# Turn between two blocks: the last down projection in two column halves, row factors applied through a diagonal matrix

## The chip, the cores and the metric

One core of one Trainium2 chip. The metric is the device time of one execution in microseconds (us); lower is better. The kernel before took 1072.19 us, the median of 3 runs (1071.92 to 1072.72).

## What is computed

Two blocks over 256 tokens of 1024 channels, in fp32. The first ends in a mixture of experts (32 experts, two per token) that adds to the residual h, and in a final normalization; the second block begins with a normalization of its own and one wide projection:

```python
# end of the first block
    out = out + jnp.einsum('nef,efd->nd', h * combine[:, g, :, None], w_down[g])
    h = h + hierarchical_moe(hn, ...)
return rmsnorm(h, final_norm_g)
# start of the second block
    h = rms_norm(x, g_mix[l])
    z = jnp.einsum("bsd,de->bse", h, w_in[l]) + b_in[l]
    va, ga, xb, gb, sa, sb = jnp.split(z, cuts, axis=-1)
```

Both normalizations are taken of the same h: the first one's factor is needed for the residual, and the factor of both together for the projection's input.

## The kernel before

The tokens lie in two row blocks of 128 (index c), as h[128, 2, 1024]. The experts are worked off in 16 pairs; each pair takes 12 weight tiles of 1 MB (4 gate, 4 up, 4 down) from a ring of buffers in six pools (a to f), which SyncE (SP) fills in the order of use as soon as a slot is freed (`Ring`, L35 to L89). Of the last down tile, the two halves of columns are separate transfers (L128).

For a pair, TensorE computes gate and up (L830), VectorE and ScalarE form hs (L705), four transposes turn it (L713), and the down projection (L960 to L966) runs k = 0 to 3 outside, the two halves of 512 columns n = 0, 1 inside, into the banks dn0 and dn1. An fp32 matmul stands as two instructions in the trace, a transpose as one. `evac` (L720) writes the result of a half as a high part y[:, 0] (ScalarE) and a low part y[:, 1] (VectorE). `to_token` (L725) multiplies them by the one-hot matrix GT, two matmuls per row block and half, and VectorE adds the result to h. For the pairs before the last this is done inside the next pair.

After the last pair comes the turn. `scattered(c, n)` (L992) adds half n of the columns to row block c; `square` (L996, ScalarE) squares it with a sum per row in s1; `weighted` (L999, VectorE) multiplies the squares by g2, the broadcast of the first norm's squared gains (plus epsilon), with a sum per row in s2; `factor(c)` (L1002) adds the two sums on VectorE (sn) and takes the power -1/2 on GpSimd (r1). Then hn = h * r1 is written for both row blocks: for c = 0 by ScalarE (L1036) and VectorE (L1040), for c = 1 by VectorE in two halves (L1122). Sixteen transposes of hn (L1130) fill four PSUM banks, and `split_x` (L1078) makes from each the high part n_hi (ScalarE, L1082) and the low part n_lo (VectorE, L1085) of the projection's input X. r0 (L1123) is the first norm's own factor, with which h is scaled at L1136 by gfin, the broadcast of the gains (L1119).

The projection (`ws`, L1088) reads its weights in units, half a tile each: `Units.split` (L213) makes w_hi on ScalarE (L228) and, in the second block up to unit 75, w_lo on GpSimd (L229). Unit 0 is split in two pieces inside the turn (L1028, L1033, L1041), unit 1 at L1120, units 2 and 3 at L1137; later ones three units ahead of their use, in four buffers. A unit is 24 matmuls; the first two projections read units 0, 1 and 2, 3. PSUM has eight banks named acc here (L1048), given out in turn.

Order. From the end of the last pair's down projection (L969) to L1142 the instructions of TensorE, VectorE, ScalarE and GpSimd stand in the order of the code (`manual_schedule`). Before it, from the third pair on, this holds for TensorE alone (L929); after it a planner orders all engines by simulated times. SP's transfers follow the frees of the ring.

Of the kernel before, what the change touches and what calls it, by code (L numbers as in the profile page):

```python
# [8 lines left out]
F32 = mybir.dt.float32  # L9
# [3 lines left out]
AF = mybir.ActivationFunctionType  # L13
OP = mybir.AluOpType
# [78 lines left out]
def kernel(ctx: ExitStack, tc: tile.TileContext, a: dict, out):  # L93
    nc = tc.nc
    V, S, T, G = nc.vector, nc.scalar, nc.tensor, nc.gpsimd
# [3 lines left out]
    small = ctx.enter_context(tc.tile_pool(name="small", bufs=2))  # L99
    NA, NB, NC, ND, NE, NF = 5, 9, 2, 2, 1, 2  # L100
    R = ctx.enter_context(tc.tile_pool(name="R", bufs=1, side="right"))
    ring = Ring(nc)
# [14 lines left out]
    W_EXP = []  # L117
# [46 lines left out]
    h = keep.tile([128, 2, 1024], F32, name="h")  # L164
# [10 lines left out]
    ident = consts.tile([128, 128], F32, name="ident")  # L175
# [10 lines left out]
    def keep_warm(n, pool, name):  # L186

        p = pool.tile([128, 512], F32, name=name)
        for _ in range(n):
            T.matmul(p, ones_b, ones_b[:, 0:1].to_broadcast([128, 512]), start=True, stop=True)  # L190

    keep_warm(12, psA, "acc")
    mhalf = consts.tile([128, 4], F32, name="mhalf")
# [85 lines left out]
    r1 = small.tile([128, 2], F32, name="r1")  # L279
    diag = p1.tile([128, 2, 128], F32, name="diag", tag="x40")  # L280
# [16 lines left out]
    for kk in range(4):  # L297
        for kt in (2 * kk, 2 * kk + 1):
            S.activation(hnh[kt // 4][:, kt % 4], pts[kt // 2][:, kt % 2].rearrange("p c t -> p (c t)"), AF.Copy,
                         scale=gcol[:, kt:kt + 1])  # L300
        for kt in (2 * kk, 2 * kk + 1):
            V.scalar_tensor_tensor(hnl[kt // 4][:, kt % 4], pts[kt // 2][:, kt % 2].rearrange("p c t -> p (c t)"),
                                   gcol[:, kt:kt + 1], hnh[kt // 4][:, kt % 4].bitcast(F32), op0=OP.mult,
                                   op1=OP.subtract)
# [355 lines left out]
    def output(tag="r4"):  # L660
        return R.tile([128, 2, 512], F32R, name="y", tag=tag)
# [26 lines left out]
    def slots(i):  # L688
        g = GS[i].rearrange("t c j s -> t c (j s)")
        p = psM.tile([128, 2, 128], F32, name="ms")  # L690
        for c in range(2):
            T.transpose(p[:, c], g[:, c], ident)
        GT[i] = mw.tile([128, 2, 128], F32R, name="onehotT")
        S.activation(GT[i], p, AF.Copy)
        p = psM.tile([128, 3], F32, name="ms")
        for c in range(2):
            T.matmul(p, g[:, c], cwr[:, c, i], start=c == 0, stop=c == 1)
        CW[i] = mw.tile([128, 2], F32, name="cw")
        done = V.tensor_copy(CW[i][:, 0:1], p[:, 2:3])
        for j in range(2):  # L700
            s = slice(64 * j, 64 * j + 64)
            V.tensor_mul(CW[i][s, 1:2], p[s, j:j + 1], CW[i][s, 0:1])
        return done
# [9 lines left out]
    def transpose_h(hs, m, hT):  # L713
        p = psM.tile([128, 4, 128], F32, name="ms")
        for k in range(4):
            turned[0] = T.transpose(p[:, k, :m], hs[:m, k], ident[:m, :m])  # L716
        V.tensor_copy(hT[:, :, :m], p[:, :, :m])
        return hT

    def evac(dn, n, m, y):  # L720

        S.activation(y[:m, 0], dn[n][:m], AF.Copy)  # L722
        V.tensor_sub(y[:m, 1], dn[n][:m], y[:m, 0].bitcast(F32))  # L723

    def to_token(gt, c, m, y):  # L725

        p = psM.tile([128, 512], F32, name="ms")
        for k in range(2):
            T.matmul(p, gt[:m, c], y[:m, k], start=k == 0, stop=k == 1)  # L729
        return p  # L730
# [185 lines left out]
    def broadcast(p, rows, n):  # L916

        for k in range(4):
            T.matmul(p[:, k], ident[:, 4 * n + k:4 * n + k + 1].to_broadcast([128, 128]), rows, start=True, stop=True)
        return p.rearrange("p k c -> p (k c)")  # L920

    prev = None
    turn = ExitStack()
    steady = ExitStack()
    for i in range(16):
        if i == 2:


            steady.enter_context(tc.manual_schedule(engines={T.engine}))  # L929
        gate = psE.tile([128, 512], F32, name="gate")  # L930
        up = psE.tile([128, 512], F32, name="up")
        if i < 15:
            onehot(i + 1)
        products(i, "w_gate", gate, XG[i])
        if prev:
            scatter_late(*prev)
        if i == 0:
            with tc.issue_after(slots(0).ins):
                param_cols()
        with tc.issue_after(tile_done[0].ins) if i == 0 else ExitStack():  # L940
            products(i, "w_up", up, XG[i], (lambda: scatter(prev[0], prev[1], 1, 128)) if prev else None)
        if i == 0:
            nb = nc.values_load(nmore_i[0:1, 0:1], min_val=0, max_val=7)
        hs_hT = hidden()
        hs = act_mul(gate, up, CW[i], 128, hs_hT[:, 0])
        rows = gather(i + 1) if i < 15 else iter(())
        next(rows, None)
        if i < 2:
            next(rows, None)
            slots(i + 1)  # L950
        hT = transpose_h(hs, 128, hs_hT[:, 1])
        if 2 <= i < 15:
            next(rows, None)
            slots(i + 1)
        if i == 15:

            with tc.issue_after(turned[0].ins):
                g2 = [broadcast(psE.tile([128, 4, 128], F32, name=n), gfin_rows2, k) for k, n in enumerate(("gate", "up"))]
        dn = [psE.tile([128, 512], F32, name=f"dn{n}") for n in range(2)]
        for k, idx in enumerate(W_EXP[i]["w_down"]):  # L960
            t = ring.get(idx)
            for n in range(2):
                for j in range(2):
                    m = T.matmul(dn[n][64 * j:64 * j + 64], hT[:, k, 64 * j:64 * j + 64], t[:, j, 512 * n:512 * n + 512],  # L964
                             start=k == 0, stop=k == 3, skip_group_check=True)
            ring.free(idx)  # L966
        if i == 15:
            steady.close()
            turn.enter_context(tc.manual_schedule(engines={T.engine, V.engine, S.engine, G.engine}))  # L969
        y = output()  # L970
        evac(dn, 0, 128, y)
        prev = (GT[i], y, dn, 128)
        if i == 1:
            scatter_late(*prev)
            scatter(GT[i], y, 1, 128)
            prev = None
            overflow()
    y2 = output("r2")
    evac(dn, 1, 128, y2)

    s1 = small.tile([128, 2, 2], F32, name="s1")
    s2 = small.tile([128, 2, 2], F32, name="s2")
    floor = small.tile([128, 1], F32, name="floor")
    V.memset(floor, 1024 * EPS * EPS)
    sn = small.tile([128, 2], F32, name="sn")
    r0 = small.tile([128, 2], F32, name="r0")
    r1 = small.tile([128, 2], F32, name="r1")
    sqs = [R.tile([128, 2, 512], F32, name=f"sq2{c}", tag=("r3", "r1")[c]) for c in range(2)]  # L990

    def scattered(c, n):  # L992
        s = slice(512 * n, 512 * n + 512)
        V.tensor_add(h[:, c, s], h[:, c, s], to_token(prev[0], c, 128, (y, y2)[n]))

    def square(c, n):  # L996
        S.activation(sqs[c][:, n], h[:, c, 512 * n:512 * n + 512], AF.Square, accum_out=s1[:, c, n:n + 1])

    def weighted(c, n):  # L999
        V.scalar_tensor_tensor(sqs[c][:, n], sqs[c][:, n], 1.0, g2[n], op0=OP.mult, op1=OP.mult, accum_out=s2[:, c, n:n + 1])  # L1000

    def factor(c):  # L1002
        V.scalar_tensor_tensor(sn[:, c:c + 1], s2[:, c, 0:1], s2[:, c, 1:2], floor, op0=OP.add, op1=OP.add)
        G.tensor_tensor(r1[:, c:c + 1], sn[:, c:c + 1], mhalf[:, 0:1], op=OP.pow)

    ring.close("b")
    ring.close("c")
    ring.close("d")
# [10 lines left out]
                  + [(W_2[j], half) for j in (14, 15) for half in range(2)])  # L1019
    U = {unit: u for u, unit in enumerate(units2.seq)}  # L1020

    hn = q0.tile([128, 2, 1024], F32, name="hn", tag="t8")
    scattered(0, 0)
    square(0, 0)
    scattered(0, 1)
    square(0, 1)
    weighted(0, 0)
    low = units2.split(2)  # L1028
    scattered(1, 0)
    square(1, 0)  # L1030
    scattered(1, 1)
    square(1, 1)
    low.pop(0)()  # L1033
    weighted(0, 1)
    factor(0)
    S.activation(hn[:, 0, 512:1024], h[:, 0, 512:1024], AF.Copy, scale=r1[:, 0:1])  # L1036
    weighted(1, 0)
    weighted(1, 1)
    factor(1)
    V.tensor_scalar(hn[:, 0, 0:512], h[:, 0, 0:512], r1[:, 0:1], None, op0=OP.mult)  # L1040
    for step in low:  # L1041
        step()
    phase.close()


# [71 lines left out]
                nc.sync.dma_start(w[p0:p0 + hi - lo, :, c0:c0 + 96], src)  # L1117

    gfin = [broadcast(psP.tile([128, 4, 128], F32, name="acc"), gfin_rows, n) for n in range(2)]  # L1119
    units2.prep(1)  # L1120
    for n in range(2):
        V.tensor_scalar(hn[:, 1, 512 * n:512 * n + 512], h[:, 1, 512 * n:512 * n + 512], r1[:, 1:2], None, op0=OP.mult)  # L1122
    V.tensor_add(r0, s1[:, :, 0], s1[:, :, 1])  # L1123
    rms_scale(r0, r0, 1024)
    pt = [psP.tile([128, 2, 2, 128], F32, name="acc") for kk in range(4)]
    for c, kks in ((0, (2, 3, 0, 1)), (1, range(4))):
        for kk in kks:
            for k in range(2):
                kt = 2 * kk + k
                T.transpose(pt[kk][:, k, c], hn[:, c, 128 * kt:128 * kt + 128], ident)  # L1130
    for kk in range(4):
        split_x(X, pt[kk], PC["g_mix"], kk)
    for c in range(2):
# [384 lines left out]
```

## Time and profile before

| | us |
|---|---|
| median of 3 runs | 1072.19 |
| the profiled execution | 1072.1 |
| its span, first to last instruction | 1070.4 |
| TensorE busy in it | 1031.7 (96%) |
| VectorE busy | 544.5 (51%) |
| ScalarE busy | 369.3 (34%) |
| GpSimd busy | 221.4 (21%) |

TensorE's mean granted clock is 0.985 of full speed. The experts take the span from about 120 to 580 us, the turn lies at 570 to 596, the second block behind it. In the rows PE is a matmul on TensorE, PEld its weight load, DVE is VectorE, ACT ScalarE, POOL GpSimd, SPq the queue of SyncE. Times are us from the start of the span unless marked ns. L12 is line 12 of the kernel; where a helper issues the instruction it is the helper's line. Matmuls overlap, so the sum of their durations is more than the time that they take.

### The profile page before, as it was taken

To read this page: it belongs to the slowest core of one execution; us is meant where nothing else is said; L and a number is where in the kernel's file an instruction comes from. 1 tells how busy PE (TensorE), PEld (TensorE's weight loads), DVE (VectorE), ACT (ScalarE), POOL (GpSimd) and SP (SyncE) were. 2 spreads that over 40 slices of the span, in tenths; PEclk is the share of its full clock that TensorE was granted. 3 is DMA by queue.
4 is the path that set the end of the run, shared out by engine and by line. 5 is a ranking of instruction groups with operands and counts; after the bars stand their busy time and mean duration, and the time that the engine had idled before them with its cause. 6 is when DMAs were issued, how large, how long until landed. Compare 5 with 4: busy or idle time off the path is not lost.

```text
span 1070.4 us, 16246 instructions
## 1 busy us (share of the span) xinstructions
PE 1031.7 (96%) x6624; PEld 740.3 (69%) x6624; DVE 544.5 (51%) x1025; ACT 369.3 (34%) x596; POOL 221.4 (21%) x123
## 2 busy tenths in 40 slices
PE   8999998999999999999998899989897999999997
PEld 7998644444444444444444898869897999998996
DVE  4758433122222222222224889897986366555555
ACT  5565211000000000000002545866536445445443
POOL 0161000000000000000001887454885800000000
PEclk9999999999999999999999999989898999999999
DMA  9997899899999999999999664423462665655531
GB/s 315 301 358 278 311 368 410 339 409 409 408 409 410 409 409 409 409 408 409 409 409 368 190 196 160 133 88 117 158 197 95 193 206 185 205 181 180 195 117 40
DMA packets 138987, 299.70 MB, mean 280 GB/s; under 512 B 14325, under 2 KB 79325, under 8 KB 138909
## 3 DMA queue, kind: packets, MB, share of 16 engines
q1 hardware_dynamic: 138397, 297.32, 75.8%
q8 instruction: 53, 0.87, 0.3%
q10 hardware_dynamic: 432, 1.05, 0.2%
q0 software_dynamic: 80, 0.26, 0.1%
q14 instruction: 25, 0.20, 0.1%
HBM read 297.56 MB, written 1.05 MB: 279 GB/s over the span
## 4 chain that ended last, share of the span: by engine, by line
PE 72%; DVE 5%; issue 2%; POOL 1%; ACT 1%; POOLq 0%; DVEq 0%; ACTq 0%
PE acc L1096 22%; PE up L830 9%; PE dn L964 9%; PE gate L830 9%; PE acc L1416 8%; PE ms L676 5%; PE ms L729 3%; PE acc L1389 2%; PE acc L1347 2%; DVE acc L1158 1%; POOL w_lo L229 1%; PE acc L1224 1%; PE ms L716 1%; DVE vb L1247 1%; PE acc L1220 1%
## 5 line engine op out<-in xcount | busy, mean ns | idle before, releaser
L229 POOL TENSOR_TENSOR w_lo<-ring_a,w_hi 128x1024 fp32r<-128x1024 f32 (+1 forms) x77 | 186.4, 2437 | 535.3 <-ACT w_hi L228 534.4
L228 ACT ACTIVATE w_hi<-ring_a 128x1024 fp32r<-128x1024 f32 (+1 forms) x169 | 169.1, 1004 | 131.6 <-PE acc L1096 39.1
L229 DVE TENSOR_TENSOR w_lo<-ring_a,w_hi 128x1024 fp32r<-128x1024 f32 (+1 forms) x92 | 101.7, 1108 | 71.1 <-ACT w_hi L228 71.1
L1096 PE MATMUL acc<-n_hi,w_hi 128*128 128x256 f32 x448 | 119.3, 293 | 7.3 <-DVE rg L1236 4.6
L1096 PE MATMUL acc<-n_hi,w_lo 128*128 128x256 f32 x448 | 118.0, 290 | 1.8 <-POOL w_lo L229 1.8
L1158 DVE SCALAR_TENSOR_TENSOR acc<-ub,pcol,acc 128x256 f32<-128x256 f32 x232 | 104.0, 481 | 5.5 <-issue 2.8
L735 DVE TENSOR_TENSOR h<-h,ms 128x512 f32<-128x512 f32 x60 | 38.5, 683 | 125.7 <-PE ms L729 125.7
L722 ACT ACTIVATE y<-dn 128x512 fp32r<-128x512 f32 x32 | 19.0, 597 | 227.1 <-PE dn L964 113.0
L1096 PEld LDWEIGHTS acc<-n_hi,w_hi 128*128 128x128 f32 x448 | 88.2, 197 | 10.4 <-ACT acc L1229 4.7
L1096 PEld LDWEIGHTS acc<-n_hi,w_lo 128*128 128x128 f32 x448 | 88.1, 197 | 2.1 <-POOL w_lo L229 2.1
L723 DVE TENSOR_TENSOR y<-dn,y 128x512 fp32r<-128x512 f32 x32 | 21.9, 687 | 119.6 <-ACT y L722 119.6
L1096 PE MATMUL acc<-n_lo,w_hi 128*128 128x256 f32 x448 | 82.5, 286 | 0.0
L676 PEld LDWEIGHTS ms<-onehot,x_moe 128*128 128x128 f32 x512 | 59.9, 192 | 14.8 <-issue 13.0
L1096 PEld LDWEIGHTS acc<-n_lo,w_hi 128*128 128x128 f32 x448 | 66.9, 194 | 0.0
L676 PE MATMUL ms<-onehot,x_moe 128*128 128x128 f32 x512 | 64.4, 279 | 0.8 <-DVE onehot L666 0.8
L1096 PE MATMUL acc<-x2h,w_hi 128*128 128x256 f32 x256 | 64.6, 280 | 0.0
L1096 PE MATMUL acc<-x2h,w_lo 128*128 128x256 f32 x256 | 64.5, 281 | 0.0
L964 PE MATMUL dn<-ring_b,hs_hT 128*64 128x512 f32 x240 | 57.0, 597 | 0.0
L1416 PE MATMUL acc<-w_hi,fh 128*128 128x512 f32 x128 | 50.1, 391 | 0.0
L1416 PE MATMUL acc<-w_lo,fh 128*128 128x512 f32 x128 | 49.9, 390 | 0.0
L1416 PE MATMUL acc<-w_hi,fl 128*128 128x512 f32 x128 | 49.5, 391 | 0.0
L1096 PEld LDWEIGHTS acc<-x2h,w_hi 128*128 128x128 f32 x256 | 48.3, 189 | 0.6
(368 smaller groups left out, 2017.1 us busy)
## 6 DMA issues: line engine op xcount, KB each, us to landing
ring_a<-in_w_in_dram SPq DMA_DIRECT2D x32, 1024.0 KB, 9.1
ring_a<-in_w_dram SPq DMA_DIRECT2D x32, 1024.0 KB, 5.5
ring_b<-in_w_down_dram SPq DMA_DIRECT2D x30, 1024.0 KB, 18.4
ring_b<-in_w_gate_dram SPq DMA_DIRECT2D x26, 1024.0 KB, 18.3
ring_b<-in_w_up_dram SPq DMA_DIRECT2D x25, 1024.0 KB, 18.3
ring_a<-in_w_gate_dram SPq DMA_DIRECT2D x18, 1024.0 KB, 14.5
ring_a<-in_w_up_dram SPq DMA_DIRECT2D x15, 1024.0 KB, 12.1
ring_a<-in_w_down_dram SPq DMA_DIRECT2D x14, 1024.0 KB, 18.6
```

The costliest lines, as they stand in the source:

```text
L228: S.activation(hi[:, s], src[:, s], AF.Copy)
L229: steps.append(lambda s=s: E.tensor_sub(lo[:, s], src[:, s], hi[:, s].bitcast(F32)))
L676: T.matmul(p[:, k], xp[c][:, 128 * (k0 + k):128 * (k0 + k + 1)], g[:, c], start=c == 0, stop=c == 1)
L723: V.tensor_sub(y[:m, 1], dn[n][:m], y[:m, 0].bitcast(F32))
L729: T.matmul(p, gt[:m, c], y[:m, k], start=k == 0, stop=k == 1)
L735: V.tensor_add(h[:, c, s], h[:, c, s], to_token(gt, c, m, y))
L830: m = T.matmul(ps[64 * j:64 * j + 64, :], x[:, 2 * q + k, 64 * j:64 * j + 64], t[:, j, 512 * k:512 * k + 512], start=q == 0 and k == 0, st ...
L964: m = T.matmul(dn[n][64 * j:64 * j + 64], hT[:, k, 64 * j:64 * j + 64], t[:, j, 512 * n:512 * n + 512], start=k == 0, stop=k == 3, skip_gr ...
L1096: T.matmul(ps[:, b, :], w[:, k, b * 128:(b + 1) * 128], xx[4 * half + k], start=half == 0 and b == 0 and k == 0 and w is wh and not low, s ...
L1158: V.scalar_tensor_tensor(ca[:, j] if k == 30 else s, ub[:, j, k:k + 256], conv_a_w[:, 8 * k + j:8 * k + j + 1], s, op0=OP.mult, op1=OP.add)
L1347: T.matmul(pb[b // 2][:, b % 2, :], w[:, kk, b * 128:(b + 1) * 128], xx[:, kt], start=kt == 0 and b % 2 == 0 and q == 0, stop=kt == 11 and ...
L1416: T.matmul(out_ps[c][n], f[:, half, 128 * c:128 * c + 128], w[:, 0, 512 * n:512 * n + 512], start=j == 0 and half == 0 and q == 0, stop=j ...
```

## The change

The last pair leaves the loop after its transposes. Its g2 goes into the banks dn0, dn1, ahead of these transposes. The down projection runs with the halves of columns outside and k inside, into the banks gate and up; inside its second half, before k = 2, stand scatter, square and weighted of the first half for both row blocks. The ring's slots are freed in the second half. Then come the second half's scatter, square and weighted, and the factors. hn is gone: a 128 x 128 diagonal matrix of each row block's factor is written on VectorE (diag, by `ident` times r1), and sixteen fp32 matmuls of h by diag take the place of the sixteen transposes of hn. Eight warming matmuls (bf16, 512 columns, result unused; `keep_warm`, L186) are put in front of them, in an acc bank of their own. Both pieces of unit 0's low part are put ahead of the first factor on GpSimd.

```diff
@@ -919,6 +919,39 @@
             T.matmul(p[:, k], ident[:, 4 * n + k:4 * n + k + 1].to_broadcast([128, 128]), rows, start=True, stop=True)
         return p.rearrange("p k c -> p (k c)")
 
+    s1 = small.tile([128, 2, 2], F32, name="s1")
+    s2 = small.tile([128, 2, 2], F32, name="s2")
+    floor = small.tile([128, 1], F32, name="floor")
+    sn = small.tile([128, 2], F32, name="sn")
+    r0 = small.tile([128, 2], F32, name="r0")
+    r1 = small.tile([128, 2], F32, name="r1")
+    sqs = []
+    def scattered(c, n):
+        s = slice(512 * n, 512 * n + 512)
+        V.tensor_add(h[:, c, s], h[:, c, s], to_token(GT[15], c, 128, ys[n]))
+    def square(c, n):
+        S.activation(sqs[c][:, n], h[:, c, 512 * n:512 * n + 512], AF.Square, accum_out=s1[:, c, n:n + 1])
+    def weighted(c, n):
+        V.scalar_tensor_tensor(sqs[c][:, n], sqs[c][:, n], 1.0, g2[n], op0=OP.mult, op1=OP.mult, accum_out=s2[:, c, n:n + 1])
+    def factor(c):
+        V.scalar_tensor_tensor(sn[:, c:c + 1], s2[:, c, 0:1], s2[:, c, 1:2], floor, op0=OP.add, op1=OP.add)
+        G.tensor_tensor(r1[:, c:c + 1], sn[:, c:c + 1], mhalf[:, 0:1], op=OP.pow)
+    def first_half():
+        for c in range(2):
+            scattered(c, 0)
+        for c in range(2):
+            square(c, 0)
+        for c in range(2):
+            weighted(c, 0)
     prev = None
     turn = ExitStack()
     steady = ExitStack()
@@ -948,14 +981,15 @@
         if i < 2:
             next(rows, None)
             slots(i + 1)
+        if i == 15:
+            g2 = [broadcast(psE.tile([128, 4, 128], F32, name=f"dn{k}"), gfin_rows2, k) for k in range(2)]
         hT = transpose_h(hs, 128, hs_hT[:, 1])
         if 2 <= i < 15:
             next(rows, None)
             slots(i + 1)
         if i == 15:
-            with tc.issue_after(turned[0].ins):
-                g2 = [broadcast(psE.tile([128, 4, 128], F32, name=n), gfin_rows2, k) for k, n in enumerate(("gate", "up"))]
+            break
         dn = [psE.tile([128, 512], F32, name=f"dn{n}") for n in range(2)]
         for k, idx in enumerate(W_EXP[i]["w_down"]):
             t = ring.get(idx)
@@ -964,9 +998,6 @@
                     m = T.matmul(dn[n][64 * j:64 * j + 64], hT[:, k, 64 * j:64 * j + 64], t[:, j, 512 * n:512 * n + 512],
                              start=k == 0, stop=k == 3, skip_group_check=True)
             ring.free(idx)
-        if i == 15:
-            steady.close()
-            turn.enter_context(tc.manual_schedule(engines={T.engine, V.engine, S.engine, G.engine}))
         y = output()
         evac(dn, 0, 128, y)
         prev = (GT[i], y, dn, 128)
@@ -975,34 +1006,26 @@
             scatter(GT[i], y, 1, 128)
             prev = None
             overflow()
-    y2 = output("r2")
-    evac(dn, 1, 128, y2)
-    s1 = small.tile([128, 2, 2], F32, name="s1")
-    s2 = small.tile([128, 2, 2], F32, name="s2")
-    floor = small.tile([128, 1], F32, name="floor")
+    steady.close()
+    turn.enter_context(tc.manual_schedule(engines={T.engine, V.engine, S.engine, G.engine}))
     V.memset(floor, 1024 * EPS * EPS)
-    sn = small.tile([128, 2], F32, name="sn")
-    r0 = small.tile([128, 2], F32, name="r0")
-    r1 = small.tile([128, 2], F32, name="r1")
-    sqs = [R.tile([128, 2, 512], F32, name=f"sq2{c}", tag=("r3", "r1")[c]) for c in range(2)]
-    def scattered(c, n):
-        s = slice(512 * n, 512 * n + 512)
-        V.tensor_add(h[:, c, s], h[:, c, s], to_token(prev[0], c, 128, (y, y2)[n]))
-    def square(c, n):
-        S.activation(sqs[c][:, n], h[:, c, 512 * n:512 * n + 512], AF.Square, accum_out=s1[:, c, n:n + 1])
-    def weighted(c, n):
-        V.scalar_tensor_tensor(sqs[c][:, n], sqs[c][:, n], 1.0, g2[n], op0=OP.mult, op1=OP.mult, accum_out=s2[:, c, n:n + 1])
-    def factor(c):
-        V.scalar_tensor_tensor(sn[:, c:c + 1], s2[:, c, 0:1], s2[:, c, 1:2], floor, op0=OP.add, op1=OP.add)
-        G.tensor_tensor(r1[:, c:c + 1], sn[:, c:c + 1], mhalf[:, 0:1], op=OP.pow)
+    sqs += [R.tile([128, 2, 512], F32, name=f"sq2{c}", tag=("r3", "r1")[c]) for c in range(2)]
+    dn = [psE.tile([128, 512], F32, name=n) for n in ("gate", "up")]
+    ys = [output("r2")]
+    for n in range(2):
+        for k, idx in enumerate(W_EXP[15]["w_down"]):
+            if (n, k) == (1, 2):
+                first_half()
+            t = ring.get(idx)
+            for j in range(2):
+                T.matmul(dn[n][64 * j:64 * j + 64], hT[:, k, 64 * j:64 * j + 64], t[:, j, 512 * n:512 * n + 512],
+                         start=k == 0, stop=k == 3, skip_group_check=True)
+            if n == 1:
+                ring.free(idx)
+        if n == 1:
+            ys.append(output())
+        evac(dn, n, 128, ys[n])
     ring.close("b")
     ring.close("c")
     ring.close("d")
@@ -1019,27 +1042,19 @@
                   + [(W_2[j], half) for j in (14, 15) for half in range(2)])
     U = {unit: u for u, unit in enumerate(units2.seq)}
 
-    hn = q0.tile([128, 2, 1024], F32, name="hn", tag="t8")
-    scattered(0, 0)
-    square(0, 0)
+    diag = q0.tile([128, 2, 128], F32, name="diag2")
+    low = units2.split(2)
     scattered(0, 1)
     square(0, 1)
-    weighted(0, 0)
-    low = units2.split(2)
-    scattered(1, 0)
-    square(1, 0)
     scattered(1, 1)
     square(1, 1)
-    low.pop(0)()
-    weighted(0, 1)
-    factor(0)
-    S.activation(hn[:, 0, 512:1024], h[:, 0, 512:1024], AF.Copy, scale=r1[:, 0:1])
-    weighted(1, 0)
-    weighted(1, 1)
-    factor(1)
-    V.tensor_scalar(hn[:, 0, 0:512], h[:, 0, 0:512], r1[:, 0:1], None, op0=OP.mult)
     for step in low:
         step()
+    for c in range(2):
+        weighted(c, 1)
+        factor(c)
+        if c == 0:
+            V.tensor_scalar(diag[:, 0], ident, r1[:, 0:1], None, op0=OP.mult)
     phase.close()
 
 
@@ -1117,17 +1132,15 @@
                 nc.sync.dma_start(w[p0:p0 + hi - lo, :, c0:c0 + 96], src)
 
     gfin = [broadcast(psP.tile([128, 4, 128], F32, name="acc"), gfin_rows, n) for n in range(2)]
+    keep_warm(8, psP, "acc")
     units2.prep(1)
-    for n in range(2):
-        V.tensor_scalar(hn[:, 1, 512 * n:512 * n + 512], h[:, 1, 512 * n:512 * n + 512], r1[:, 1:2], None, op0=OP.mult)
+    V.tensor_scalar(diag[:, 1], ident, r1[:, 1:2], None, op0=OP.mult)
     V.tensor_add(r0, s1[:, :, 0], s1[:, :, 1])
     rms_scale(r0, r0, 1024)
     pt = [psP.tile([128, 2, 2, 128], F32, name="acc") for kk in range(4)]
-    for c, kks in ((0, (2, 3, 0, 1)), (1, range(4))):
-        for kk in kks:
-            for k in range(2):
-                kt = 2 * kk + k
-                T.transpose(pt[kk][:, k, c], hn[:, c, 128 * kt:128 * kt + 128], ident)
+    for c in range(2):
+        for kt in range(8):
+            T.matmul(pt[kt // 2][:, kt % 2, c], h[:, c, 128 * kt:128 * kt + 128], diag[:, c], start=True, stop=True)
     for kk in range(4):
         split_x(X, pt[kk], PC["g_mix"], kk)
     for c in range(2):
```

## Rows read from the trace of the kernel before

**Rows 1.** Chain that ended last, 555 to 680 us: start us, us, what

```profile
572.54 7.04 PE dn L964 x32
...
588.09 3.98 DVE hn L1122 x2
...
593.22 66.41 PE acc L1096 x552
```

**Rows 2.** Timeline of GpSimd and VectorE, 588 to 592: start us, us, engine, line, operation

```profile
588.02 1.26 POOL L229 TENSOR_TENSOR w_lo<-ring_a,w_hi 128x512 fp32r<-128x512 f32 x1
...
588.09 1.48 DVE L1122 TENSOR_SCALAR hn<-h,r 128x512 f32<-128x512 f32 x1 [0.45 <-POOL r L1004]
...
589.25 2.52 POOL L229 TENSOR_TENSOR w_lo<-ring_a,w_hi 128x1024 fp32r<-128x1024 f32 x1
...
589.49 2.57 DVE L1122 TENSOR_SCALAR hn<-h,r 128x512 f32<-128x512 f32 x1
```

**Rows 3.** Two single lines: duration in ns (minimum/median/maximum), first and last start

```profile
L285 DVE TENSOR_SCALAR diag<-ident,r x2: 286/288/290, 6.6 to 8.1; 128x128 f32<-128x128 f32 x2
...
L1040 DVE TENSOR_SCALAR hn<-h,r x1: 480/480/480, 587.2 to 587.2; 128x512 f32<-128x512 f32 x1
```

**Rows 4.** Stretches: length, busy PE PEld DVE ACT POOL (instructions), granted clock, DMA share, GB/s

```profile
569.00:572.00 3.00, 2.08 (x19) 1.91 (x18) 1.58 (x3) 0.00 (x0) 0.00 (x0) 1.00 1.02 399
572.00:576.00 4.00, 4.00 (x23) 1.60 (x24) 0.00 (x0) 0.00 (x0) 0.00 (x0) 1.00 1.06 371
...
590.00:592.00 2.00, 0.28 (x3) 0.04 (x1) 2.00 (x2) 1.57 (x4) 1.77 (x1) 0.93 0.06 19
592.00:593.00 1.00, 0.89 (x5) 0.89 (x5) 0.97 (x5) 0.17 (x1) 0.59 (x1) 0.50 0.15 18
...
730.00:755.00 25.00, 20.39 (x167) 19.89 (x166) 22.08 (x32) 15.31 (x21) 14.84 (x7) 0.94 0.26 85
```

**Rows 5.** Timeline of TensorE: the first and the eleventh matmul of the second block

```profile
592.88 0.56 PE L1096 MATMUL acc<-n_hi,w_hi 128*128 128x256 f32 x1
...
595.15 0.28 PE L1096 MATMUL acc<-n_hi,w_hi 128*128 128x256 f32 x1
```

**Rows 6.** Timeline of the turn, 567 to 604; idle time before in brackets, and what ended it

```profile
570.10 0.66 PE L716 MATMUL ms<-ident,hs_hT 128*128 128x128 f32 x4 [0.92 <-DVE hs_hT L707]
...
579.60 1.09 ACT L722 ACTIVATE y<-dn 128x512 fp32r<-128x512 f32 x2 [13.29 <-PE dn L964]
580.23 1.29 DVE L723 TENSOR_TENSOR y<-dn,y 128x512 fp32r<-128x512 f32 x2 [8.61 <-ACT y L722]
...
581.52 1.28 DVE L994 TENSOR_TENSOR h<-h,ms 128x512 f32<-128x512 f32 x2
...
582.24 0.63 ACT L997 ACTIVATE sq<-h 128x512 f32<-128x512 f32 x1 [1.55 <-DVE h L994]
...
583.00 0.69 DVE L1000 SCALAR_TENSOR_TENSOR sq<-sq,gate 128x512 f32<-128x512 f32 x1 [0.20 <-ACT sq L997]
...
584.35 2.05 PE L919 MATMUL acc<-gfin_rows,ident 128*128 128x128 f32 x16 [1.33 <-DVE h L994]
...
585.55 0.22 DVE L1003 SCALAR_TENSOR_TENSOR sn<-s,floor 128x1 f32<-128x1 f32 x1
...
585.85 0.58 POOL L1004 TENSOR_TENSOR r<-sn,mhalf 128x1 f32<-128x1 f32 x1 [0.39 <-DVE sn L1003]
...
590.10 1.57 ACT L1082 ACTIVATE n_hi<-acc,pcol 128x256 fp32r<-128x256 f32 x4 [1.96 <-PE acc L1130]
...
594.27 2.02 ACT L228 ACTIVATE w_hi<-ring_a 128x1024 fp32r<-128x1024 f32 x2
...
595.42 9.47 POOL L229 TENSOR_TENSOR w_lo<-ring_a,w_hi 128x1024 fp32r<-128x1024 f32 x4 [2.32 <-ACT w_hi L228]
```

**Rows 7.** A weight tile's transfer: the timeline of SP's queue; KB, us to landing

```profile
547.65 1.99 SPq L79 DMA_DIRECT2D ring_f<-in_w_up_dram  x1
...
ring_f<-in_w_up_dram SPq DMA_DIRECT2D x1, 1024.0 KB, 18.2
```

## The prediction

> **What bounds the kernel now.** I read the chain of work that ended last, first. From 572.54 us TensorE runs the last experts' down projection for 7.04 us, and from 593.22 the second block's first projection for 66.41 us (552 matmuls, 0.120 each) [rows 1]. Between them the chain leaves TensorE and runs through ScalarE, VectorE and GpSimd: that turn, some 14 us, is all that the change touches. Its dearest piece is VectorE's hn at L1122, 3.98 us for two instructions [rows 1].
>
> The timelines of GpSimd and VectorE show why. The two halves of row block 1 take 1.48 and 2.57 us, while the same operation on the same shape took 0.48 us at L1040 [rows 2, 3]. GpSimd's w_lo pieces ran from 588.02 to 589.28 and from 589.25 to 591.77; each hn ended 0.29 us after the piece beside it [rows 2]. So such a VectorE instruction (SBUF to SBUF, one tensor and a scalar per row) is held until the GpSimd instruction in progress ends. GpSimd starts its split right behind the pow that VectorE waits for, and was first by 0.07 us.
>
> The table by stretches adds a second cost: the granted clock falls between 590 and 592, where TensorE was busy for only 0.28 of 2 us, and is 0.50 (1.2 GHz) after it [rows 4]. The first matmuls of the second block pay: ten in 2.27 us, 592.88 to 595.15 [rows 5], instead of 1.20. At full clock the stream would have had to start at 593.95 to be where it is. That is the mark against which the new turn is measured: 593.95, not 592.88.
>
> **The change part by part.** *g2 ahead of the transposes of hs.* TensorE waits 0.92 us before those transposes, from 569.18 [rows 6], and g2's new banks (dn0, dn1) were emptied an expert earlier. Eight fp32 broadcasts are 16 instructions; 16 of that form took 2.05 us with their tail [rows 6], 0.111 each, so g2 ends at 570.96, the transposes (0.66) at 571.62, VectorE's copy (about 0.66, as its other operations of 128x512) at 572.3. The down projection starts at 572.4, before at 572.5: nothing gained, nothing lost.
>
> *Down projection by column halves.* 32 instructions 0.21 apart, the last of a group ending 0.59 after its start (7.04 in all). The first half ends at 572.4 + 15 x 0.21 + 0.59 = 576.14; y's high part (ScalarE, 0.61) and low part (VectorE, 0.64) (halves of the pairs in [rows 6]) are ready by 577.45, just as TensorE has issued k = 0, 1 of the second half (577.44). The four scatter matmuls take 0.84 and 0.1 of waiting, with k = 2, 3 queued behind them; these end at 580.44, where all ended at 579.58. So 0.86 us is paid, and bought with it: scatter, add, square and weighted of columns 0 to 511 are done beside TensorE by about 581.1, just as y's second high part is ready (581.07).
>
> *Second half to the factors.* y's low part ends at 581.73. Then, with the distances of the trace before, 0.66 to the add, 0.71 to the square, 0.76 to weighted, 0.72 to sn, 0.30 to the pow of 0.58 [rows 6]: the pow of block 0 runs from 584.88 to 585.46. The diag of block 0 follows on VectorE at 585.49 and takes 0.29, as at L285 [rows 3], since GpSimd has only the second pow queued. weighted(1,1) stands behind it: 585.80, then 0.72, 0.30 and 0.58: the second pow ends at 587.40. Before, it ended at 588.07, so this part brings 0.67.
>
> *The second diag* replaces 3.98 us of hn. GpSimd's next instruction is the split of unit 1 (its ScalarE half lies done), 2.37 us, as four took 9.47 [rows 6], and diag is of the held kind. Bounds: not held, 0.29, ready at 587.7; held throughout, 587.37 + 2.37 + at most 0.29 = 590.0. I take held, nearest to [rows 2], with a tail of 0.10 for 128 columns: 589.85, 2.45 after the pow, where hn was ready 4.00 after it. VectorE's r0 and the low parts of X wait behind it, and need block 1's matmuls anyway.
>
> *Transposing through the diagonal.* Block 0's eight matmuls (16 instructions, 1.78) stand in front: g_fin from 583.1 (third add done) to 584.9, the eight warming matmuls (0.21 each, as others of 512 columns) to 586.6, block 0 to 588.4. All of that is hidden under the wait for diag; without that cover it is the bound (rival A). Block 1's 16 instructions run from 589.9 to 591.7: 1.85 from diag to the stream, where four transposes took 0.81. As TensorE is dense from 583.1 to 588.4, I take the full clock behind.
>
> The rows price an fp32 matmul at two instructions of 0.111 each, a transpose at one. The Trainium skill (TensorE: Matmul & The Clock Gate, Terms) calls transpose mode four times faster for fp32; by that, block 1 would take 3.55 and the sum be 1.8 us worse. No row shows that factor; the broadcasts show two.
>
> *Waiting for data.* w_down's last tile comes in two column halves. A w_up tile issued at 547.65 landed 18.2 us later [rows 7], at 565.9; behind it stand k = 0, 1, 2 (1.05 MB each) and the first half of k = 3: 3.67 MB at 399 down to 371 GB/s [rows 4]: 575.1 to 575.8. It was read at 577.5, and would now be at 574.9: a wait of 0 to 0.9; I take 0.15, as the rate was highest at the start. The second half is read after 579. The ring's slots come free 1 to 2 us later, so SP issues three w_in tiles later; they are wanted behind units 2 and 3, split from 594.27 [rows 6], which hides that.
>
> *After the turn.* ScalarE's eight n_hi at 0.39 from 590.6, unit 2's w_hi (1.0), then 2.37 on GpSimd [rows 6] give 597.3; wanted at 591.85 + 48 x 0.12 = 597.6. It just fits. The second projection now takes g_fin's first bank, free at about 596.5 when VectorE has scaled h, and wanted at 597.6: hidden too.
>
> **Sum.** 0.67 (up to the second pow) + 1.55 (4.00 of hn against 2.45 of diag) - 1.04 (1.85 against 0.81 for transposing) + 1.07 (clock) - 0.15 (data) = 2.1 us. The stream behind is bound by TensorE and what it feeds, so the shift stays. The profiled execution took 1072.1 (span 1070.4): 1070.0; the median of the runs is 0.09 above it: 1070.1.
>
> **Rivals.** *A: diag isn't held* (VectorE comes first, or 128 columns slip through). Block 1 then follows block 0 at 588.4 and the stream starts at 590.35: 3.6 us, 1068.6. Against it: [rows 2], where GpSimd was first. Chance 0.13.
>
> *B: the last weight tile binds*, waited for whole or landing a microsecond late: TensorE stands 1.4 us at k = 3 of the first half: 1071.4. For it: the margin is nil [rows 7]; against it: the halves are separate transfers. Chance 0.15.
>
> *C: the clock falls anyway* in the 1.5 us of waiting for diag. [...] For it: [rows 4], where it fell after thin work; against it: the work before this wait is dense. The Trainium skill (same page, Part 4: PE-mode transpose) says that transposes don't count as work for the clock in the same way. Only transposes ran before the fall, so the trace doesn't contradict it; by it the new matmuls hold the clock and this rival goes. Chance 0.08.
>
> *D: the second block is ordered otherwise.* Behind the turn the order is planned from simulated times, which the change shifts. Between 730 and 755 TensorE stands 4.6 of 25 us [rows 4], in a chain of unit splits. Each split put one step back there costs a w_hi and a w_lo, 1.0 + 2.37 = 3.4 us: one gives 1073.5, two give 1076.9. It makes the kernel slower from 2.1 us of added standing on, by over 0.2% from 4.2 on. Chance 0.10, and 0.04 for the same with the sign turned (one fewer, 1066.7). The profile speaks for neither.
>
> That the change doesn't do what it says I leave out: the hn instructions go.
>
> **Numbers.** Forecast 0.50, A 0.13, B 0.15, C 0.08, D 0.14. A measurement here tells 0.2% (2.1 us) from no change; the forecast lies on that bound, so half of it counts as faster: 0.25 + 0.13 + 0.04 = 0.42. Within: 0.25 + 0.15 + 0.08 = 0.48. Slower: 0.10. The range goes from A (1068.2, with 0.4 to spare) to B and C with the bounds of diag and data on top (1072.6); D lies outside.
>
> **What would show it.** Right: the second pow ending near 587.4; behind it a diag of about 2.4 us beside a w_lo of 2.4; the first matmul of block 2 near 591.9 at clock 1.00, 0.12 apart from the start. Wrong: a diag of 0.3 us there (A); a gap in the down matmuls at k = 3 (B); 0.50 after 590 (C); a shift at 593 that is gone by 755 (D). If the down matmuls end after 581, my order of that work is wrong.

## The result, and the profile after

The kernel after took 1076.85 us (median of six runs, 1076.08 to 1077.96), the kernel before on the same chip 1071.85: ratio 1.0052, 95% interval 1.0041 to 1.0063. It is slower by 5 us; the forecast was 1070.1. The two profiled executions differ by as much: spans of 1070.4 and 1075.8.

A cut at the end of the second block's first 552 matmuls splits these 5.4 us. Before, they end at 593.22 + 66.41 = 659.63 [rows 1]. The chain that ended last, 555 to 680 us, of the kernel after (start us, us, what):

```profile
572.62 3.68 PE gate L1022 x16
...
585.48 0.59 POOL r L945
...
587.04 1.16 PE acc L919 x8
588.20 3.26 PE acc L190 x8
591.46 3.72 PE acc L1143 x32
595.17 65.50 PE acc L1111 x552
```

They end at 660.67: **the turn costs 1.0 us** where it should have brought 2.1 (0.2 of it stands ahead: the experts' up projection ends at 569.37 instead of 569.20). Behind the cut, before needs 410.8 us to the end of its span and after 415.1: **another 4.3 us come from the second block**, where no line was changed.

**The turn.** Up to the first pow the chain is the one that was forecast. Behind it the chain doesn't go through the second pow and diag, as it should, but over VectorE's weighted to TensorE, and stays there: a broadcast, the warming matmuls (L190), all 32 diagonal instructions. The timeline of the kernel after says why:

```profile
583.71 1.16 PE L919 MATMUL acc<-gfin_rows,ident 128*128 128x128 f32 x8 [0.32 <-DVE h L935]
...
586.29 0.68 DVE L941 SCALAR_TENSOR_TENSOR sq<-sq,dn 128x512 f32<-128x512 f32 x1
...
587.04 1.16 PE L919 MATMUL acc<-gfin_rows,ident 128*128 128x128 f32 x8 [2.17 <-DVE sq L941]
587.32 0.56 POOL L945 TENSOR_TENSOR r<-sn,mhalf 128x1 f32<-128x1 f32 x1 [1.26 <-DVE sn L944]
587.84 2.34 POOL L229 TENSOR_TENSOR w_lo<-ring_a,w_hi 128x1024 fp32r<-128x1024 f32 x1
587.91 2.35 DVE L1137 TENSOR_SCALAR diag<-ident,r 128x128 f32<-128x128 f32 x1 [0.67 <-POOL r L945]
...
588.03 3.42 PE L190 MATMUL acc<-ones_b 128*128 128x512 bf16 x8
...
591.25 3.93 PE L1143 MATMUL acc<-diag,h 128*128 128x128 f32 x32
...
594.93 0.37 PE L1111 MATMUL acc<-n_hi,w_hi 128*128 128x256 f32 x1
```

The second g_fin broadcast writes an acc bank which is the very bank that held the second half of g2 (the tile dn1). The last reader of g2 is weighted(1, 1), at 586.29. TensorE, whose instructions stand in the order of the code here, stood 2.17 us for it, with the warming and both row blocks' matmuls queued behind, although block 0's diag was ready at 586.38. The stretches of the kernel after (length, busy PE, PEld, DVE, ACT, POOL, granted clock, DMA share, GB/s) show what followed:

```profile
586.00:588.00 2.00, 0.96 (x8) 0.96 (x9) 1.20 (x5) 0.00 (x0) 0.74 (x3) 1.00 1.10 347
588.00:590.00 2.00, 2.00 (x8) 0.76 (x8) 2.00 (x1) 0.00 (x0) 2.00 (x1) 0.56 0.73 240
590.00:592.00 2.00, 2.00 (x10) 1.36 (x9) 0.51 (x3) 0.00 (x0) 0.89 (x2) 0.59 0.38 95
592.00:593.00 1.00, 1.00 (x11) 1.00 (x10) 0.00 (x0) 0.00 (x0) 0.00 (x0) 1.00 1.05 369
```

Behind the stand the granted clock was near 0.5 (1.2 GHz) for most of 588 to 592, and the eight warming matmuls, whose result nobody reads, took 0.43 each instead of 0.21. The clock was full when the stream began, behind 3.4 us of warming on TensorE; whether the warming earned that is tested below.

**The second block.** What TensorE waited for from 660 us on, in the kernel before (us in total, times, longest):

```profile
PE acc L1096 <- DVE rg L1236: 4.6, 1, 4.6
PE acc L1096 <- ACT w_hi L228: 2.8, 1, 2.8
PE acc L1096 <- POOL w_lo L229: 1.8, 1, 1.8
...
PE acc L1306 <- DVE part L1297: 0.5, 1, 0.5
```

and in the kernel after:

```profile
PE acc L1233 <- DVE vb L1214: 6.5, 1, 6.5
...
PE acc L1111 <- ACT w_hi L228: 3.0, 1, 3.0
PE acc L1111 <- POOL w_lo L229: 3.0, 2, 1.8
PE acc L1319 <- DVE part L1310: 1.8, 1, 1.8
```

These sum to 9.7 and 14.3, which accounts for the 4.3 within half a us (the rows left out are alike, 5.3 and 5.4, 1.0 and 1.0). Of these rows the longest has another cause than before: TensorE stands until 714.69 for vb, the last step of a convolution on VectorE. It stands 1.9 us longer there than before for rg; 1.4 more go to the unit splits (w_lo, w_hi) and 1.3 to part. The order of the instructions behind the turn differs: in the traces at least 16 of TensorE's 3306 matmul records, 22 of VectorE's 551 and 7 of ScalarE's 369 stand elsewhere, with 12 loads of activation tables where there were 10. VectorE now works through steps of another convolution (L1171) ahead of that last step.

### The profile page after: what moved, and what is told of

Its sections match the earlier page's. It is cut to its first block, busy times and chain, and to the rows that moved or that the text cites. A ratio compares the mean times of both kernels' runs of the same rounds, so it can differ in the third digit from the quotient of the medians.

```text
span 1075.8 us, 16293 instructions
## 1 busy us (share of the span) xinstructions
PE 1035.2 (96%) x6648; PEld 740.2 (69%) x6648; DVE 546.3 (51%) x1024; ACT 371.3 (35%) x597; POOL 221.8 (21%) x123
## 4 chain that ended last, share of the span: by engine, by line
PE 71%; DVE 5%; issue 2%; ACT 2%; POOL 1%; POOLq 0%; ACTq 0%; DVEq 0%
PE acc L1111 21%; PE up L830 9%; PE gate L830 9%; PE dn L998 8%; PE acc L1429 8%; PE ms L676 5%; PE ms L729 3%; PE acc L1402 2%; PE acc L1360 2%; DVE acc L1171 1%; POOL w_lo L229 1%; DVE vb L1260 1%; PE ms L716 1%; DVE part L1310 0%; PE acc L1237 0%
## 5 line engine op out<-in xcount | busy, mean ns | idle before, releaser
L1171 DVE SCALAR_TENSOR_TENSOR acc<-ub,pcol,acc 128x256 f32<-128x256 f32 x232 | 105.0, 482 | 5.9 <-issue 2.8
```

The source lines that it names most:

```text
L1171: V.scalar_tensor_tensor(ca[:, j] if k == 30 else s, ub[:, j, k:k + 256], conv_a_w[:, 8 * k + j:8 * k + j + 1], s, op0=OP.mult, op1=OP.add)
```

## The experiments

Some of these nine kernels add or drop warming matmuls, whose result is unused. Each time stands with its ratio to the kernel before on the same chip.

### The order of the second block

The order is planned from simulated times. With ten warming matmuls instead of eight, it comes out exactly as in the kernel before; everything else stays.

```diff
-    keep_warm(8, psP, "acc")
+    keep_warm(10, psP, "acc")
```

> The changed kernel with ten warming matmuls instead of eight; with them the planned order of the second block is, instruction for instruction on TensorE, VectorE, ScalarE and GpSimd, the order of the kernel before. Theory P (most of the loss is the other order in the second block, two more table loads on ScalarE among it; about 4.2 of the 5.4 us of span): the turn gets longer by two matmuls at half clock, 0.85 us, the rest is given back: 1076.85 + 0.85 - 4.2 = 1073.5. Theory T (the loss is the turn's, the order costs nothing): 1077.7.

1072.62 us, ratio 1.0007 (0.9994 to 1.0020): two more matmuls made the kernel 4 us faster. So the order carries most of the loss, as theory P has it, and the turn as it ran gains nothing.

The other way round: eight warming matmuls behind g_fin in the kernel before bring a third order there (at least 16, 24 and 7 of the same records elsewhere, 12 table loads).

```diff
+    keep_warm(8, psP, "acc")
     units2.prep(1)
```

> The kernel before with eight warming matmuls behind its gfin broadcasts and nothing else; the planned order of the second block becomes like that of the changed kernel (twelve table loads in it instead of ten). Theory P: the turn gains up to 1.1 us (the clock stays up) and the order costs about 4: 1074.8 to 1076. Theory T: 1070.8 to 1071.9, no slower than before.

1071.74, ratio 0.9999 (0.9991 to 1.0008): theory P's 1074.8 to 1076 missed. Another order isn't dear as such, and neither are two more table loads: this one costs 0.8 us behind the cut (411.6 to the end). TensorE's longest wait for a convolution is 3.0 us in it. What costs is the particular order of the kernel after.

The turn itself is 0.6 us shorter here, and the clock did not fall in it, though TensorE's last wait for hn is as long as before (1.83 us). One of its stretches:

```profile
590.00:592.00 2.00, 0.17 (x2) 0.08 (x2) 1.97 (x3) 1.48 (x4) 1.59 (x1) 1.00 0.01 2
```

### The bank

Two kernels were to take the second g_fin broadcast out of the way, by moving it behind block 0's diagonal matmuls, once in each order.

```diff
-    gfin = [broadcast(psP.tile([128, 4, 128], F32, name="acc"), gfin_rows, n) for n in range(2)]
-    keep_warm(8, psP, "acc")
+    gfin = [psP.tile([128, 4, 128], F32, name="acc") for n in range(2)]
+    gfin[0] = broadcast(gfin[0], gfin_rows, 0)
+    keep_warm(8, psP, "acc")
...
+        if c:
+            gfin[1] = broadcast(gfin[1], gfin_rows, 1)
```

The second has `keep_warm(10, ...)` for the order of the kernel before.

> The changed kernel with the second gfin broadcast put behind block 0's diagonal matmuls, eight warming matmuls between the first and these; the order of the second block stays exactly the changed kernel's. Theory B (the second gfin broadcast stood for the bank of g2's second half, the clock fell there, and the warming matmuls ran at half clock on the path): first matmul of block 2 near 592.1 instead of 594.9, 1076.85 - 2.8 = 1074.0. Rival C (the clock falls in any case, for the thin work at 580 to 584): half clock from about 588, block 1's diagonal matmuls at 0.22, start near 594, 1076.0.

> The run before this one in the list with ten warming matmuls instead of eight, with which the second block's order is exactly that of the kernel before. Theories P and B together: 1074.0 - 4.2 = 1069.8, faster than the kernel before by about 2 us; the two warming matmuls more are hidden under the wait for diag. P alone (B wrong): 1073. B alone (the order costs nothing): 1074.

1078.06, ratio 1.0063 (1.0048 to 1.0077), and 1071.69, ratio 0.9999 (0.9991 to 1.0008); 1074.0 and 1069.8 had been expected. The edit missed its aim: the warming, now the second to write an acc bank, stood 2.17 and 2.16 us for the same weighted(1, 1). One row of each timeline:

```profile
587.23 3.40 PE L190 MATMUL acc<-ones_b 128*128 128x512 bf16 x8 [2.17 <-DVE sq L941]
...
588.18 3.29 PE L190 MATMUL acc<-ones_b 128*128 128x512 bf16 x10 [2.16 <-DVE sq L941]
```

So the wait goes with the bank, not with the broadcast: the warming reads constants alone. What the bank costs these two can't say, as neither freed the turn. On the order they repeat the first pair: the tail behind the cut is 414.9 and 409.0.

So the turn was freed in another way: the halves of g2 exchange their banks, so that the bank which is wanted first is the one read out first, and the warming writes into g_fin's own first tile, ahead of the broadcasts. Block 0's matmuls start with kt = 2.

```diff
-            g2 = [broadcast(psE.tile([128, 4, 128], F32, name=f"dn{k}"), gfin_rows2, k) for k in range(2)]
+            g2 = [broadcast(psE.tile([128, 4, 128], F32, name=f"dn{1 - k}"), gfin_rows2, k) for k in range(2)]
...
-    gfin = [broadcast(psP.tile([128, 4, 128], F32, name="acc"), gfin_rows, n) for n in range(2)]
-    keep_warm(8, psP, "acc")
+    gfin = [psP.tile([128, 4, 128], F32, name="acc") for n in range(2)]
+    keep_warm(10, psP, "acc", gfin[0].rearrange("p k c -> p (k c)"))
+    gfin = [broadcast(gfin[n], gfin_rows, n) for n in range(2)]
```

> The changed kernel with g2's two halves in exchanged banks, so that the second gfin broadcast takes the bank of g2's first half (read for the last time near 581.5), and the warming matmuls (ten) ahead of both broadcasts, in a bank of their own data; the order of the second block is exactly that of the kernel before. Theory B (TensorE stood for g2's bank, and that standing dropped the clock): no wait for weighted(1,1) any more, clock 1.00 throughout, block 1's diagonal matmuls follow diag at 590.3, first matmul of block 2 near 592.1 after up's end at 569.4 (22.7 us, against 25.5 in the changed kernel): 2.8 us less than e1 would have without its two matmuls more: 1069 to 1070.5. Theory F (later standing of the second block swallows what the turn gains or loses): end within 1 us of the kernel before, 1071 to 1072.

1069.38, ratio 0.9977 (0.9968 to 0.9986): faster than both kernels, in the order of the kernel before, as theory B has it. Its timeline:

```profile
585.20 2.34 PE L189 MATMUL acc<-ones_b 128*128 128x512 bf16 x10 [0.31 <-DVE h L934]
...
587.37 1.95 PE L918 MATMUL acc<-gfin_rows,ident 128*128 128x128 f32 x16
...
587.78 0.68 DVE L940 SCALAR_TENSOR_TENSOR sq<-sq,dn 128x512 f32<-128x512 f32 x1
...
589.15 1.95 PE L1143 MATMUL acc<-diag,h 128*128 128x128 f32 x16
589.33 2.35 POOL L228 TENSOR_TENSOR w_lo<-ring_a,w_hi 128x1024 fp32r<-128x1024 f32 x1
589.39 2.36 DVE L1137 TENSOR_SCALAR diag<-ident,r 128x128 f32<-128x128 f32 x1 [0.67 <-POOL r L944]
...
591.81 2.05 PE L1143 MATMUL acc<-diag,h 128*128 128x128 f32 x16 [0.71 <-DVE diag L1137]
```

The warming runs 0.21 apart, nothing waits for weighted, and the only stand behind the warming is 0.71 us for diag: the turn as the prediction drew it. Of the two edits the warming's new place does most: the second broadcast now starts at 588.26 (587.37 + 8 x 0.11), and weighted(1, 1) ends at 588.46, so in its old bank it would have stood 0.2 us, hidden under the wait for diag. Neither edit was run alone. From the end of the experts' up projection (the start of g2) to the cut it takes 88.48 us; the kernel after takes 91.30 (569.37 to 660.67). The kernel before ends its up projection at 569.20 and reaches the cut in 90.43. The freed turn gains 1.95 on before; 2.1 was forecast. The spans of the two profiled executions differ by 1.8, but not by this alone: the freed kernel's up projection ended 1.7 later and its tail is 1.6 shorter.

The same kernel with eight warming matmuls falls into the order of the kernel after.

```diff
-    keep_warm(10, psP, "acc", gfin[0].rearrange("p k c -> p (k c)"))
+    keep_warm(8, psP, "acc", gfin[0].rearrange("p k c -> p (k c)"))
```

> e5 with eight warming matmuls instead of ten, with which the second block has exactly the changed kernel's order (on ScalarE two rows differ). Theory P: the turn as in e5, and some 4 us more behind it, TensorE standing about 6.5 us for vb: 1073.5 to 1074.5. Theory T: as e5.

1075.46, ratio 1.0035 (1.0022 to 1.0048): 6.1 us slower than its twin for two matmuls that nobody needs, and above theory P's 1073.5 to 1074.5. The turn is the same (88.69); the tail is 415.6 instead of 409.2. TensorE's waits from 660 us on have the vb row of the kernel after again, which its twin lacks, and more for w_lo (1.9 in the twin):

```profile
PE acc L1233 <- DVE vb L1214: 6.4, 1, 6.4
...
PE acc L1110 <- POOL w_lo L228: 3.5, 2, 2.1
```

Waits make up some 4.3 of the 6.3 us between the tails; the rest was not traced. This pair shows the cost of the order by itself. That the misplaced steps of L1171 are what makes it dear is read from the timeline; an order written by hand was not tried.

### The warming

The kernel after without its warming matmuls:

```diff
-    keep_warm(8, psP, "acc")
```

> The changed kernel without the eight warming matmuls; the order of the second block becomes that of e2 (the kernel before with eight of them), which cost nothing there. Theory W (the warming matmuls ran at half clock on the path and earned nothing): first matmul of block 2 1 to 2 us earlier than in the changed kernel, and the order's 4 us gone: 1071 to 1072. Theory K (they are what brought the clock back before the diagonal matmuls): these run at half clock instead and the start is no earlier: 1072.5 to 1073.5.

1072.99, ratio 1.0018 (1.0008 to 1.0028), in nearly the order of the second experiment. The time lies in theory K's range, but K is wrong: the diagonal matmuls ran at full clock without the warming. Two rows of its timeline:

```profile
587.50 1.16 PE L919 MATMUL acc<-gfin_rows,ident 128*128 128x128 f32 x8 [2.16 <-DVE sq L941]
...
590.78 2.05 PE L1142 MATMUL acc<-diag,h 128*128 128x128 f32 x16 [0.34 <-DVE diag L1136]
```

and one of its stretches:

```profile
588.00:590.00 2.00, 2.00 (x20) 2.00 (x20) 1.63 (x1) 0.00 (x0) 2.00 (x2) 1.00 0.91 295
```

TensorE stood 2.16 us for g2's bank as in the kernel after, but the clock stayed at 1.00, and the turn took 88.51 us, as short as the freed one. The stand alone does little harm, since it ends before diag is ready; stand, fallen clock and eight matmuls in the way together cost 2.8. So the warming in the kernel after earned nothing. The tail, at 413.0, takes the gain back.

### The held instruction

The freed turn still has diag held for 2.36 us beside GpSimd's w_lo. On ScalarE:

```diff
-    V.tensor_scalar(diag[:, 1], ident, r1[:, 1:2], None, op0=OP.mult)
+    S.activation(diag[:, 1], ident, AF.Copy, scale=r1[:, 1:2])
```

> As the run before it in the list, with the second diag on ScalarE. Theory H (VectorE's diag is held by the split of unit 1 beside it, ScalarE's isn't): diag ready about 0.3 us after the pow instead of 2.35, block 1's matmuls follow block 0's and gfin's without a gap, first matmul of block 2 near 591.3, 0.8 us earlier than with diag on VectorE: 0.8 us less in the whole, if the second block passes it on. Rival: ScalarE's diag takes as long: no difference.

1068.25, ratio 0.9973 (0.9961 to 0.9985). Its timeline:

```profile
588.24 3.74 PE L1143 MATMUL acc<-diag,h 128*128 128x128 f32 x32
588.42 2.35 POOL L228 TENSOR_TENSOR w_lo<-ring_a,w_hi 128x1024 fp32r<-128x1024 f32 x1
588.48 0.40 ACT L1137 ACTIVATE diag<-ident,r 128x128 f32<-128x128 f32 x1 [1.93 <-POOL r L944]
```

Beside the same w_lo, ScalarE's diag takes 0.40, and the matmuls of both row blocks run without a gap. What that is worth is not shown: the interval overlaps that of the kernel with diag on VectorE, and in the profiles the turn is no shorter (88.8 against 88.5), since here the down projection waited 0.8 us for w_down:

```profile
574.43 1.08 PE L1021 MATMUL gate<-ring_a,hs_hT 128*64 128x512 f32 x4 [0.55 <-DMA ring_a<-in_w_down_dram]
575.80 1.08 PE L1021 MATMUL gate<-ring_a,hs_hT 128*64 128x512 f32 x4 [0.28 <-DMA ring_a<-in_w_down_dram]
```

Without that wait the turn would be some 0.5 shorter by this sum, not rival A's 1.5: from the warming on TensorE then stands for nothing, and its own row of work is the bound.

That raises the question what the diagonal itself is worth, since in the kernel before, too, the dear thing was a held instruction. So the last experiment leaves the whole change out, and in the kernel before moves only hn of row block 1 to ScalarE:

```diff
-        V.tensor_scalar(hn[:, 1, 512 * n:512 * n + 512], h[:, 1, 512 * n:512 * n + 512], r1[:, 1:2], None, op0=OP.mult)
+        S.activation(hn[:, 1, 512 * n:512 * n + 512], h[:, 1, 512 * n:512 * n + 512], AF.Copy, scale=r1[:, 1:2])
```

> The kernel before with one edit: both hn halves of row block 1 are written on ScalarE (as one half of row block 0 already is, 0.72 us) instead of VectorE. Transposes, column order, order of the second block: as before. Theory H (the dear thing in the turn of the kernel before was the hold of VectorE beside GpSimd's split, not the form of the transposing): hn takes 2 x 0.72 from about 588.15 on ScalarE, behind the w_hi of 1.04; it is ready at 589.6 instead of 592.06, the second block's first matmul starts 2.0 to 2.5 us earlier (about 590.6 to 590.9), the fall of the clock costs about 1 us as before, and the median is 1068.7 to 1069.3, as short as the freed turn with the diagonal (1068.25 to 1069.38). Rival R (the diagonal, the column halves and the warming are needed for the gain): ScalarE is late for w_hi of unit 1 or for n_hi, the start moves by less than 0.7 us, and the median stays within 1070.5 to 1071.5.

1068.17, ratio 0.9965 (0.9953 to 0.9976), in the order of the kernel before, and below theory H's range. Its timeline:

```profile
588.06 3.62 POOL L229 TENSOR_TENSOR w_lo<-ring_a,w_hi 128x512 fp32r<-128x512 f32 x2
588.12 1.34 ACT L1122 ACTIVATE hn<-h,r 128x512 f32<-128x512 f32 x2
...
588.90 1.27 PE L1130 MATMUL acc<-ident,hn 128*128 128x128 f32 x8 [0.51 <-ACT hn L1122]
...
589.93 0.37 PE L1096 MATMUL acc<-n_hi,w_hi 128*128 128x256 f32 x1
590.01 0.19 PEld L1096 LDWEIGHTS acc<-n_hi,w_lo 128*128 128x128 f32 x1
590.13 0.28 PE L1096 MATMUL acc<-n_hi,w_lo 128*128 128x256 f32 x1
```

hn takes 1.34 us instead of 3.98 [rows 1], the stream starts at 589.93 instead of 592.88 [rows 5] and runs 0.12 apart at once. One row of its stretches:

```profile
590.00:592.00 2.00, 2.00 (x19) 2.00 (x18) 1.75 (x5) 2.00 (x7) 2.00 (x2) 1.00 0.24 83
```

Where the clock fell in the kernel before [rows 4], it is full here, and the gap before the transposes is gone (waits for hn of 3.1 us in all became 0.5). That the gap let it fall is argued, not shown: with warming in front, the second experiment had the gap and the full clock. The full clock is the part which theory H had missed, and the gain is 3.0 by the medians, 3.7 by the ratio, instead of 1.8 to 2.4. The cut comes at 590.17 + 65.56 = 655.73, and the tail is 410.9, as in the kernel before: here the whole shift stays. Theory H holds. One line gives what the change gives at its best; the intervals of this kernel and of the freed turn with diag on ScalarE overlap. In the whole time the diagonal, the column halves and the warming earn nothing that these runs can tell.

The profiles side by side: the turn from the end of the experts' up projection to the cut, and the tail from the cut to the end (us).

| kernel | turn | tail | order behind the turn | ratio |
|---|---|---|---|---|
| before | 90.4 | 410.8 | before | 1 |
| hn on ScalarE | 86.5 | 410.9 | before | 0.9965 |
| before, 8 warming | 89.8 | 411.6 | third | 0.9999 |
| after | 91.3 | 415.1 | after | 1.0052 |
| after, 10 warming | 92.3 | 408.6 | before | 1.0007 |
| after, no warming | 88.5 | 413.0 | third | 1.0018 |
| broadcast moved, 8 warming | 92.3 | 414.9 | after | 1.0063 |
| broadcast moved, 10 warming | 92.6 | 409.0 | before | 0.9999 |
| freed, 10 warming | 88.5 | 409.2 | before | 0.9977 |
| freed, 10 warming, diag on ScalarE | 88.8 | 408.4 | before | 0.9973 |
| freed, 8 warming | 88.7 | 415.6 | after | 1.0035 |

The tails group by order. Within the order of the kernel before they are about 2 us shorter in the four kernels with the diagonal than in the two that transpose hn, which makes up for the longer turn; why stays open.

## Why the prediction was wrong, step by step

- **What bounds the turn: right.** The VectorE instruction beside GpSimd's split is held. diag took 2.35 us, 2.45 had been taken from the pow on (2.38 measured, 587.88 to 590.26); where it isn't held, block 0's took 0.29, as forecast [rows 2, 3]. The Trainium skill (SBUF — State Buffer, Summary: rules for kernel authors) says of a VectorE instruction in a 2-port mode and a GpSimd instruction at the same time that the second to issue is blocked entirely until the first has finished. The rows agree: diag began 0.07 after w_lo and ended 0.08 after it; that diag runs in such a mode no row tells.
- **Up to the second pow: right within 0.5.** Forecast 587.40, measured 587.88; TensorE's down matmuls ended at 581.04, 0.6 later than worked out and just past the 581 that the prediction had set as a sign against its order. The order is as drawn: the projection began 0.2 later, and the four scatter matmuls took 1.13 instead of 0.94. No wait for the last weight tile stands in the kernel after (0.15 was taken). In the profile of the freed turn with diag on ScalarE it is 0.8 in two pieces: the bounds of 0 to 0.9 [rows 7] were good.
- **"All of that is hidden under the wait for diag": wrong.** Each piece was costed by its length and by what it reads, not by the bank that it writes. The second broadcast waited for g2's last reader until 587.04, so all but the first broadcast of the row of work that was to end at 588.4 began there.
- **"I take the full clock behind": wrong in its reason.** TensorE was not dense before the wait for diag, and the clock fell at 588. This is rival C's fall on other instructions: the warming itself ran at half clock, 3.42 us instead of 8 x 0.21. What the fall would cost block 1's matmuls no run shows. Nor did matmuls in place of transposes hold the clock by themselves: TensorE ran no transpose after 571.8. The 1.07 us of the sum did come (the stream ran 0.12 apart from its start), but that is luck as far as the reason goes: without the warming the clock stayed full, too. The stream began at 594.93, 0.98 behind the mark of 593.95; the forecast 591.85 was missed by 3.08.
- **"The shift stays": wrong.** This is rival D, and it decided. Its reason was right (simulated times move, the order flips); its place was so in part only: unit splits make 1.4 of the 4.6 us of added waits, and the longest wait is now for a convolution of VectorE, until 714.69. That its prices of 3.4 and 6.8 lie around the 4.3 of the profiles and the 6.1 of the pair of kernels is chance. Its chance of 0.10 was too low for a plan that two warming matmuls can turn, and the range left it out.

With the warming out of the wait for the bank and the order kept, the sum comes out: 2.1 forecast, 1.95 measured in the freed turn's profile.

## What to carry to other kernels

An instruction that "waits for nothing" can wait for the bank that it writes: ask who read that bank last, above all for filler work in front of a critical wait. Where a planner orders the rest, compare the two orders of instructions first: a difference there can outweigh the edit, and a kernel that keeps the old order measures the edit alone. And before an operation is rebuilt because one instruction in it is slow, see why it is slow: here moving it to an engine that isn't held brought as much as the best form of the rebuilding, in one line.

## What was not expected of the hardware

After a stand of TensorE of 2.16 to 2.17 us in front of the same bank the clock fell in the kernel after and stayed at 1.00 in the kernel without warming. What tells these apart stays open; each is one execution.

The same small operation beside the same GpSimd instruction took 2.36 us on VectorE and 0.40 on ScalarE.
